# Attention scores of 64-feature heads as two 64-row matmuls into two PSUM banks, keys no longer block-diagonal

## Chip, cores and metric

One core of one Trainium2 chip runs the program. The metric is the device time of one execution in microseconds; lower is better. The time before is 1701.77 us, the median of 3 runs (1701.06 to 1705.58).

## What is computed

Two transformer blocks are applied, one after the other, to 256 tokens of 1024 features, all in float32. The first block is a hybrid mixer (a chunked state-space scan beside a "forgetting" attention of 8 heads) and a mixture of 16 experts. The second block has two layers, each with a mixer of three attentions, a cross attention and a gated feed-forward. What matters here are the four attentions with heads of 64 features; a query row of 128 tokens looks at 128 or 256 keys:

```
forgetting:  logits = einsum('bqhd,bkhd->bhqk', q, k) * 64**-0.5 + fcum[q] - fcum[k]    # block 1, 8 heads
window:      s = einsum('bqgrd,bkgd->bgrqk', qb, kb) * 64**-0.5                         # block 2, each layer:
             p = masked_probs(s, mask, sink)      # SWA, window 128, with a sink        # 8 heads, 2 key groups
             o_sel, o_win                         # NSA, selected and window, gated     # 2 x 8 heads, 2 key groups
             mla_mixer: heads of 96 features      # not touched by the layout below
             x = x + merged @ w_out ; x = x + cross_attn(...) ; x = x + ffn(...)
```

With 256 tokens each attention is plain causal attention over one or two blocks of 128 keys (SWA also masks the keys that are 128 or more behind).

## The kernel before, in words

Everything is written in straight Python on one `Build` object; a scheduler then orders the instructions of each engine. It goes by the order in which they are written and by when an operand or a buffer is free in its own model, so matmuls of a later projection are put between those of an attention. Every engine then takes its own instructions strictly in that order. SBUF work tiles are pages of 4, 2 and 1 KB per partition, taken and given back in turn (`a`, `f`; `PAGES` says how many). PSUM has 8 banks: two for projections (`lin`), two for scores (`S`), one each for transposes (`tp`) and outputs (`o`), two for the rest (`m`).

Projections (`linA`, `linB`, `mm3`, L161 to L163) split each float32 operand into a high and a low float32r part and make three matmuls of it. The attention matmuls are plain float32, and the trace shows each of them as two records on TensorE.

`attn` (L391) serves one group of four heads. It makes the scores in three fills of an `S` bank: four heads for the first 128 queries (four times 128 keys), then heads 0 and 1, then heads 2 and 3 for the second 128 queries (twice 256 keys). `qkpairs` (L422) makes the scores of two heads in one matmul of 128 contraction rows (L427): the queries of two heads lie in the two halves of the partitions, and the keys stand in a block-diagonal tile, head one's keys in rows 0 to 63 of one column block, head two's in rows 64 to 127 of the next, with zeros elsewhere. The zeros are set by GpSimd (`newdiag`, L1458 and L1459; L845 and L846 in `mixer1`) and the keys are put in by two copies of ScalarE (`kdiag`, L1452 and L1453; L852 and L853). A matmul of a bf16 identity with a mask closes each fill (L407, in SWA also L405). `smax` (L352) takes row maxima (L357), exponentials with their sums (L364), reciprocals (L371) and the scaling (L374); `ptile` transposes the probabilities (L383); the outputs are matmuls of 64 columns (L416 to L418), even heads into PSUM partitions 0 to 63, odd heads into 64 to 127.

`attn` runs 18 times: 2 calls in `mixer1` (with 8-row matmuls that add the forget sums, L867), and in each layer of `mixer2` 2 for MLA, 2 for SWA and 4 for NSA. All but the four of MLA go through `qkpairs`: 14 calls with 4 matmuls each.

Of the kernel before, what the change touches and what calls it, by code (L numbers as in the profile page):

```python
# [16 lines left out]
P = 128  # L17
# [23 lines left out]
_add("stri", (_i[:, None] < _i[None, :]))  # L41
_add("iota", np.broadcast_to(_i, (P, P)))
# [6 lines left out]
_add("gidx", np.broadcast_to(np.array([0.0, 1.0, 2.0, 3.0]), (P, 4)))  # L49
# [16 lines left out]
class Build:  # L66
    PAGES = {4: 21, 2: 7, 1: 5}
# [283 lines left out]

    def smax(self, S, nh, nk, nsink=None, gate=None):  # L352

# [6 lines left out]
        page = self.a(2, "pr")  # L360
        pr = page[:, :nh * nk].rearrange("p (a b) -> p a b", a=nh)
# [30 lines left out]
    def attn(self, qk, V, out, first=True, nsink=None, gate=None, swa=False):  # L392

        nc = self.nc
        mk = lambda m, n: m.rearrange("p (a b) -> p a b", a=4)[:, 0:n, :]
        PTs = {}
        for i, heads in ((0, (0, 1, 2, 3)), (1, (0, 1)), (1, (2, 3))):
            nk = (i + 1) * P  # L400
            nh = len(heads)
            S = self.bank("S", "S")[:, :nh * nk].rearrange("p (a b) -> p a b", a=nh)
            qk(S, heads, i, nk)
            if swa and i == 1:
                nc.tensor.matmul(S[:, :, 0:P], self.identb, self.smaskb.rearrange("p (a b) -> p a b", a=2), start=False, stop=False,  # L405
                                 skip_group_check=True)
            nc.tensor.matmul(S[:, :, i * P:nk], self.identb, mk(self.cmaskb, nh), start=False, stop=True, skip_group_check=True)  # L407
            h0 = heads[0]
            page, pr = self.smax(S, nh, nk, None if nsink is None else nsink[:, h0:h0 + nh], None if gate is None else gate(i, h0, nh))
            PTs[i, h0] = self.ptile(pr, nh, i + 1, "s" if h0 else "v")  # L410
            self.f(page)
        o = out()
        for h in range(4):
            q = o[(h % 2) * 64:(h % 2) * 64 + 64, h // 2, :]
            P0, P1 = PTs[0, 0][1], PTs[1, h // 2 * 2][1]
            nc.tensor.matmul(q[:, 0:P], V(h, 0), P0[:, h, :], start=first and h < 2, stop=True, skip_group_check=True)  # L416
            nc.tensor.matmul(q[:, P:T], V(h, 0), P1[:, h % 2, 0:P], start=False, stop=False, skip_group_check=True)
            nc.tensor.matmul(q[:, P:T], V(h, 1), P1[:, h % 2, P:T], start=False, stop=True, skip_group_check=True)  # L418
        for page, _ in PTs.values():
            self.f(page)  # L420
# [93 lines left out]
    def setup2(self):  # L514
# [6 lines left out]
        self.tri, self.stri, self.iota = self.C("tri"), self.C("stri"), self.C("iota")  # L521
# [30 lines left out]
    def setup3(self):  # L552
        nc, cp = self.nc, self.cp
        mp, rr, r1, rd, d8 = self.late
        b16 = cp.tile([P, 11 * P], BF, name="b16")
        nc.vector.tensor_copy(b16[:, 0:P], self.ident)
        self.identb = b16[:, 0:P]
        o = P
        for i, (m, n) in enumerate((("cmask", 4), ("smask", 2), ("dmask", 4))):
            v = b16[:, o:o + n * P]  # L560
            nc.vector.tensor_copy(v.rearrange("p (a b) -> p a b", a=n), bc(mp[:, i * P:(i + 1) * P], 1, n))
            setattr(self, m + "b", v)
            o += n * P
# [16 lines left out]
    def ropetables(self):  # L580
# [4 lines left out]
        ang = self.small([P, 2, 48], "ang", 1)  # L585
        for t in range(2):
            nc.vector.tensor_scalar(ang[:, t, :], C("invf"), pf[:, t:t + 1], None, op0=ALU.mult)
        k = self.small([P, 2, 48], "kk", 1)
# [11 lines left out]
        sn = self.small([P, 2, 48], "sn", 1)  # L600
# [13 lines left out]
        self.rt = rt  # L614

# [119 lines left out]
    def mixer1(self):  # L735
# [56 lines left out]
        az = self.small([P, 2, 24], "az", 1)  # L792
        nc.vector.scalar_tensor_tensor(az, z, -1.0, z, op0=ALU.mult, op1=ALU.max)
        e = self.small([P, 2, 24], "e", 1)
        nc.scalar.activation(e, az, AF.Exp, scale=-1.0)
        w = self.small([P, 2, 24], "w", 1)
# [3 lines left out]
        w2 = self.small([P, 2, 24], "w2", 1)  # L800
        nc.vector.tensor_mul(w2, w, w)
        pl = self.small([P, 2, 24], "pl", 1)
# [6 lines left out]
        nc.vector.scalar_tensor_tensor(sp, pl, 2.0, z, op0=ALU.mult, op1=ALU.add)  # L809
        nc.scalar.activation(self.Aneg, self.alog, AF.Exp)  # L810
# [31 lines left out]
        kbp = [self.a(4, f"kbd{j}") for j in range(2)]  # L842
        kbd = [k.rearrange("p (a b c) -> p a b c", a=2, b=2) for k in kbp]
        for k in kbd:
            nc.gpsimd.memset(k[0:64, :, 1, :], 0.0)  # L845
            nc.gpsimd.memset(k[64:P, :, 0, :], 0.0)  # L846
# [13 lines left out]
        for g in range(2):  # L860
            pairs = self.qkpairs(lambda p, g=g: qT[:, 2 * g + p, :], lambda p, g=g: kbd[g][:, p, :, :])

            def qkf(S, heads, i, nk, g=g):
# [1040 lines left out]
```

## Time and profile before

| | |
|---|---|
| median of the runs | 1701.77 us |
| the profiled execution | 1705.38 us |
| its span, first to last instruction | 1703.6 us |
| TensorE busy with matmuls | 1605.4 us, 94% |
| VectorE / ScalarE / GpSimd busy | 992.9 / 737.2 / 230.5 us |
| score matmuls of 64-feature heads (L427) | 112 records of 9272 |

The span is read in stages: about 0 to 105 us the start, to 430 us the rest of `mixer1` (its attention at 110 to 135), to 700 us the experts, then two layers of which the first has its attentions at about 735 to 830 us and the second at about 1245 to 1355 us. Busy times are unions of records; a matmul's record runs some 0.17 us longer than it holds the array, so the pace of TensorE is read from start to start.

### The profile page before, as it was taken

The numbers are of one execution on the slowest core, as the hardware profiler recorded it, in microseconds if no ns is written. First come the engines' busy times: TensorE is split into PE (matmuls) and PEld (weight loads), VectorE is DVE, ScalarE is ACT, GpSimd is POOL, SyncE is SP. The second block draws the span as 40 slices with busy tenths as digits, with TensorE's granted clock in tenths as the row PEclk, the third lists the DMA queues.
The fourth block names the chain that finished last, engine by engine and source line by source line (L and its number), as shares of the span: only waits on it lengthen the run. The fifth ranks groups of instructions, "written<-read, shape, count | busy, mean of one in ns | idle before, by whom it ended". The sixth has DMA issues, their size and how long they took to land. (4 is left out here: it accounts for less than half of the span.)

```text
span 1703.6 us, 23516 instructions
## 1 busy us (share of the span) xinstructions
PE 1605.4 (94%) x9272; PEld 1258.5 (74%) x9288; DVE 992.9 (58%) x1505; ACT 737.2 (43%) x1282; POOL 230.5 (14%) x258
## 2 busy tenths in 40 slices
PE   6599999988999888999999999999999999999998
PEld 5579888774433236877787789987877787789986
DVE  7866775773121128677647665545777647655544
ACT  3345754341110004565444544444565544544433
POOL 3498331420000002100000000000100000000000
PEclk9798999997999999999999999999999999999999
DMA  9867256754999997634155536554524155545550
GB/s 308 302 198 254 89 166 216 244 168 168 415 385 410 362 416 276 200 93 150 53 185 198 185 113 195 183 196 129 189 75 150 59 188 186 184 130 180 191 180 25
DMA packets 181029, 340.51 MB, mean 200 GB/s; under 512 B 20608, under 2 KB 96496, under 8 KB 173232
## 3 DMA queue, kind: packets, MB, share of 16 engines
q1 hardware_dynamic: 176784, 331.29, 55.9%
q0 software_dynamic: 1936, 6.52, 1.1%
q8 instruction: 75, 1.23, 0.3%
q10 hardware_dynamic: 2192, 1.12, 0.3%
q14 instruction: 42, 0.34, 0.1%
HBM read 337.86 MB, written 1.05 MB: 199 GB/s over the span
## 5 line engine op out<-in xcount | busy, mean ns | idle before, releaser
L226 DVE TENSOR_TENSOR wlo<-raw,whi 128x1024 fp32r<-128x1024 f32 (+3 forms) x372 | 456.4, 1238 | 316.4 <-ACT whi L226 314.5
L226 ACT CAST whi<-raw 128x1024 fp32r<-128x1024 f32 (+3 forms) x372 | 375.1, 1021 | 384.7 <-PE psA L163 152.0
L161 PE MATMUL psB<-hTh,whi 128*128 128x256 f32 x896 | 255.8, 286 | 1.3 <-ACT eA L936 0.9
L162 PE MATMUL psB<-hTl,whi 128*128 128x256 f32 x896 | 255.1, 285 | 0.0
L163 PE MATMUL psB<-hTh,wlo 128*128 128x256 f32 x896 | 254.4, 284 | 0.8 <-DVE wlo L226 0.8
L161 PE MATMUL psA<-whi,hTh 128*128 128x512 f32 (+4 forms) x496 | 188.5, 380 | 2.6 <-ACT sg L977 1.9
L163 PE MATMUL psA<-whi,hTl 128*128 128x512 f32 (+4 forms) x496 | 187.3, 378 | 0.5 <-DVE hTl L226 0.5
L162 PE MATMUL psA<-wlo,hTh 128*128 128x512 f32 (+4 forms) x496 | 186.4, 376 | 0.0
L161 PEld LDWEIGHTS psB<-hTh,whi 128*128 128x128 f32 x896 | 172.2, 192 | 3.8 <-ACT eA L936 1.3
L163 PEld LDWEIGHTS psB<-hTh,wlo 128*128 128x128 f32 x896 | 172.1, 192 | 1.7 <-DVE wlo L226 1.1
L162 PEld LDWEIGHTS psB<-hTl,whi 128*128 128x128 f32 x896 | 171.9, 192 | 2.0 <-issue 1.9
L161 PEld LDWEIGHTS psA<-whi,hTh 128*128 128x128 f32 x496 | 93.8, 189 | 20.5 <-ACT sg L977 2.3
L163 PEld LDWEIGHTS psA<-whi,hTl 128*128 128x128 f32 x496 | 93.7, 189 | 19.0 <-issue 2.4
L162 PEld LDWEIGHTS psA<-wlo,hTh 128*128 128x128 f32 x496 | 93.8, 189 | 16.0 <-issue 0.7
L364 ACT ACTIVATE pr<-S,nm 128x256 f32<-128x256 f32 (+1 forms) x160 | 66.3, 426 | 59.6 <-DVE nm L357 42.1
L639 POOL TENSOR_TENSOR macc<-macc,wmod 128x512 f32<-128x512 f32 x59 | 91.4, 1551 | 1.8
L1259 DVE TENSOR_TENSOR yf<-yg,gt 128x512 f32<-128x512 f32 x16 | 11.0, 690 | 108.8 <-PE yg L1309 93.7
L162 PE MATMUL pd<-wlo,hhl 128*128 128x512 f32 x176 | 69.8, 397 | 0.0
L163 PE MATMUL pd<-whi,hhl 128*128 128x512 f32 x176 | 69.6, 395 | 0.0
L161 PE MATMUL pd<-whi,hhl 128*128 128x512 f32 x176 | 69.3, 396 | 0.0
L272 POOL TENSOR_SCALAR sse<-ssq 128x1 f32<-128x1 f32 x16 | 4.2, 262 | 443.8 <-ACT xn L270 432.6
L638 POOL TENSOR_SCALAR wmod<-wmod,cact 128x512 f32<-128x512 f32 x59 | 60.4, 1030 | 7.6 <-DMA wmod<-in_w_mod 7.6
(583 smaller groups left out, 2987.9 us busy)
## 6 DMA issues: line engine op xcount, KB each, us to landing
raw<-in_w_in SPq DMA_DIRECT2D x62, 1024.0 KB, 5.1
raw<-in_w_down SPq DMA_DIRECT2D x44, 1024.0 KB, 7.5
raw<-in_w_gate_up SPq DMA_DIRECT2D x44, 1024.0 KB, 5.1
wmod<-in_w_mod SPq DMA_DIRECT2D x48, 512.0 KB, 5.0
raw<-in_w_gate SPq DMA_DIRECT2D x22, 1024.0 KB, 8.3
wx<-in_w_up SPq DMA_DIRECT2D x32, 512.0 KB, 10.2
raw<-in_w_up SPq DMA_DIRECT2D x16, 1024.0 KB, 9.9
wx<-in_w_gate SPq DMA_DIRECT2D x20, 512.0 KB, 9.9
```

Of the source, the lines that this page charges most:

```text
L161: m(out, l[0], r[0], start=start, stop=False)
L162: m(out, l[0], r[1], start=False, stop=False)
L163: self.lastmm = m(out, l[1], r[0], start=False, stop=stop)
L226: return self.nc.scalar.copy(hi, src), self.nc.vector.tensor_sub(lo, src, hi.bitcast(F32))
L272: self.nc.gpsimd.tensor_scalar(sq[2], sq[1][:, 0:1], 1.0 / D, RMS_EPS, op0=ALU.mult, op1=ALU.add)
L364: le = nc.scalar.activation(pr[:, h, :], S[:, h, :], AF.Exp, bias=nm[:, h:h + 1], accum_out=den[:, h:h + 1])
L638: e.tensor_scalar(w, w, c, 1.0, op0=ALU.mult, op1=ALU.mult)
L639: return e.tensor_add(acc, acc, w)
L1259: nc.vector.tensor_mul(yp, y[n], gt[:, n * 512:(n + 1) * 512])
```

## The change

The keys lie in a plain tile, as the queries do: heads with even numbers in partitions 0 to 63, heads with odd numbers in 64 to 127. `qkrows` makes one matmul of 64 contraction rows for each head, and writes even heads (b = 0) into one `S` bank and odd heads (b = 1) into the other. A call of `attn` with `rows=True` therefore takes both `S` banks for the first 128 queries and both again for the second 128; the first fill is masked and normalised in two halves, which share one page of probabilities. MLA keeps the old path. `newdiag`, `kdiag` and their memsets and second copies go; the key tiles of a layer take 2 KB pages in place of 4 KB ones, and `PAGES` has 9 of 2 KB in place of 7. Masks are kept once in bf16 and repeated by a stride of zero, some small tiles move into pages, and the strict triangle of the expert ranks is dropped (its sum now counts the token itself).

```diff
-    PAGES = {4: 21, 2: 7, 1: 5}
+    PAGES = {4: 21, 2: 9, 1: 5}
...
-        for i, heads in ((0, (0, 1, 2, 3)), (1, (0, 1)), (1, (2, 3))):
...
-            S = self.bank("S", "S")[:, :nh * nk].rearrange("p (a b) -> p a b", a=nh)
-            qk(S, heads, i, nk)
...
+        for i, sets in ((0, ((0, 2, 1, 3),)), (1, ((0, 2), (1, 3)))) if rows else ((0, ((0, 1, 2, 3),)), (1, ((0, 1), (2, 3)))):
+            nk = (i + 1) * P
+            gt = gate(i) if gate else None
+            if rows:
+                SS = [self.bank("S", "S")[:, :2 * nk].rearrange("p (a b) -> p a b", a=2) for b in range(2)]
+                qk(SS, (0, 1, 2, 3), i, nk)
+                for S in SS:
+                    close(S, i, 2)
+            for n, heads in enumerate(sets):
+                nh = len(heads)
+                if rows and i == 0:
+                    page = self.a(2, "pr")
+                    pr = page.rearrange("p (a b) -> p a b", a=4)
+                    for b in range(2):
+                        self.smax(SS[b], 2, nk, nsink[:, b:4:2] if nsink is not None else None, gt[:, b:4:2] if gate else None, pr[:, 2 * b:2 * b + 2, :])
+                elif rows:
+                    page, pr = self.smax(SS[n], 2, nk, nsink[:, n:4:2] if nsink is not None else None, gt[:, n:4:2] if gate else None)
...
-    def qkpairs(self, qT, kbd):
+    def qkrows(self, qT, kT):
 
         def qk(S, heads, i, nk):
-            for n, p in enumerate(sorted({h // 2 for h in heads})):
-                self.nc.tensor.matmul(S[:, 2 * n:2 * n + 2, :], qT(p)[:, i * P:(i + 1) * P], kbd(p)[:, :, 0:nk],
-                                      start=n == 0, stop=False, skip_group_check=True)
+            for p in range(2):
+                for b in range(2):
+                    c = slice(b * 64, b * 64 + 64)
+                    self.nc.tensor.matmul(S[b][:, p, :], qT(p)[c, i * P:(i + 1) * P], kT(p)[c, 0:nk], start=p == 0, stop=False,
+                                          skip_group_check=True)
...
-                nc.scalar.copy(kbd[b - 2][0:64, :, 0, :], ps[0:64])
-                nc.scalar.copy(kbd[b - 2][64:P, :, 1, :], ps[64:P])
+                nc.scalar.copy(kT[:, 2 * b - 4:2 * b - 2, :], ps)
...
-        self.kdiag(k, dst, t)
+        pt = self.bank("m", "tpk")[:, :T].rearrange("p (a b) -> p a b", a=2)
+        for g in range(2):
+            self.nc.tensor.transpose(pt[:, g, :], k[:, g * P:(g + 1) * P], self.ident)
+        self.nc.scalar.copy(dst.rearrange("p (a b) -> p a b", a=2)[:, :, t * P:(t + 1) * P], pt)
...
-        kaD = self.newdiag("kaD")
+        kaD = self.a(2, "kaD")
...
-        ksD, kwD = self.newdiag("ksD"), self.newdiag("kwD")
+        ksD, kwD = self.a(2, "ksD"), self.a(2, "kwD")
```

The new order of the instructions shows what the scheduler makes of it. On TensorE, in `mixer1`, the first call of `attn` stood like this before (S_915, S_941 are the first two fills of scores, kbd0 the block-diagonal keys, cfT the forget sums, b16 the identity and masks):

```order
L427 MATMUL S_915<-kbd0_602,qT_601 128x256 x2
L867 MATMUL S_915<-cfT_585,idt_70 128x128 x4
L407 LDWEIGHTS b16_542
L407 MATMUL S_915<-b16_542 128x512
L427 MATMUL S_941<-kbd0_602,qT_601 128x512
L867 MATMUL S_941<-cfT_585,idt_70 128x256 x2
```

and stands like this now (S_902 and S_903 are the two banks of the first 128 queries, S_938 and S_939 those of the second; where "..." stands, two rows like the two above it are left out, then again two, one weight load, and last 16 matmuls of the next projection):

```order
L451 MATMUL S_902<-kT_596,qT_595 128x128
L451 MATMUL S_903<-kT_596,qT_595 128x128
...
L880 MATMUL S_902<-cfT_579,idt_70 128x128
L880 MATMUL S_903<-cfT_579,idt_70 128x128
...
L406 MATMUL S_902<-b16_542 128x256
L406 LDWEIGHTS b16_542
L406 MATMUL S_903<-b16_542 128x256
...
L451 MATMUL S_938<-kT_596,qT_595 128x256 x2
L451 MATMUL S_939<-kT_596,qT_595 128x256 x2
L383 MATMUL tp_931<-idt_70,pr_914 128x128 x2
```

Here the matmuls of the two banks follow each other, without another instruction between them. On TensorE, in the NSA attention of the first layer (the window keys kwD, first 128 queries; pcmp is a small 64-row product, tp a transpose of probabilities), the order before was:

```order
L427 MATMUL S_8194<-kwD_7681,brT_7799 128x256
L1700 MATMUL pcmp_8078<-w2_8015,sv8_8076 128x64
L427 MATMUL S_8194<-kwD_7681,brT_7799 128x256
L383 MATMUL tp_8152<-idt_70,pr_8144 128x128 x4
L407 LDWEIGHTS b16_542
L407 MATMUL S_8194<-b16_542 128x512
```

and it is now, at the same fill (S_8238 and S_8239 are the two banks; psA1 is a projection):

```order
L451 MATMUL S_8238<-kwD_7718,brT_7832 128x128 x2
L406 LDWEIGHTS b16_542
L406 MATMUL S_8238<-b16_542 128x256
L159 MATMUL psA1_8512<-whi_8519,hTh0_6618 128x512
L160 MATMUL psA1_8512<-wlo_8520,hTh0_6618 128x512
L451 MATMUL S_8239<-kwD_7718,brT_7832 128x128 x2
L383 MATMUL tp_8199<-idt_70,pr_8191 128x128 x4
L406 LDWEIGHTS b16_542
L406 MATMUL S_8239<-b16_542 128x256
```

Here the two banks come apart: the even heads are done, masked and followed by a projection before the odd heads begin. Outside the attentions the order of TensorE, VectorE, ScalarE and GpSimd is that of before, but for a few weight loads in `mixer1` that change places.

## Rows read from the trace of the kernel before

**Rows 1.** The page: busy time, and the span in 40 slices.
```profile
PE 1605.4 (94%) x9272; PEld 1258.5 (74%) x9288; DVE 992.9 (58%) x1505; ACT 737.2 (43%) x1282; POOL 230.5 (14%) x258
...
PE   6599999988999888999999999999999999999998
...
PEclk9798999997999999999999999999999999999999
DMA  9867256754999997634155536554524155545550
```
**Rows 2.** Busy time by stage: window, its length, engines (records), clock, DMA share, GB/s.
```profile
105.00:165.00 60.00, 58.99 (x382) 49.35 (x382) 37.62 (x51) 30.48 (x64) 51.84 (x43) 0.94 0.62 200
...
720.00:820.00 100.00, 97.94 (x631) 75.92 (x636) 74.40 (x180) 61.02 (x176) 4.39 (x8) 1.00 0.37 119
...
1240.00:1360.00 120.00, 117.95 (x766) 88.67 (x770) 88.75 (x207) 66.11 (x197) 2.18 (x3) 1.00 0.31 98
```
**Rows 3.** One line: the score matmuls, duration ns min/median/max, forms (rows*columns).
```profile
L427 PE MATMUL S<-kaD,qaT x32: 377/486/697, 748.6 to 1269.8; 128*128 128x256 f32 x16, 128*128 128x512 f32 x16
...
L427 PE MATMUL S<-kwD,brT x32: 379/537/697, 806.5 to 1345.2; 128*128 128x256 f32 x16, 128*128 128x512 f32 x16
...
L427 PE MATMUL S<-kbd,qT x16: 378/487/592, 110.1 to 127.1; 128*128 128x256 f32 x8, 128*128 128x512 f32 x8
```
**Rows 4.** Timeline, NSA: start us, us, engine, line; a row merges its records.
```profile
796.40 1.03 PE L427 MATMUL S<-ksD,brT 128*128 128x256 f32 x4
...
797.75 1.02 PE L427 MATMUL S<-ksD,brT 128*128 128x512 f32 x2
```
**Rows 5.** One line: the 8-row matmuls of the forget sums.
```profile
L867 PE MATMUL S<-cfT,idt x32: 270/373/478, 111.1 to 128.4; 8*128 8x128 f32 x16, 8*128 8x256 f32 x16
```
**Rows 6.** Timeline of TensorE, SWA: a projection, then output matmuls of 64 columns.
```profile
757.32 0.40 PE L162 MATMUL psA<-wlo,hTh 128*128 128x512 f32 x1
757.56 0.40 PE L163 MATMUL psA<-whi,hTl 128*128 128x512 f32 x1
757.79 0.40 PE L161 MATMUL psA<-whi,hTh 128*128 128x512 f32 x1
758.12 0.32 PE L417 MATMUL oT<-PT,va 128*64 128x128 f32 x1
758.13 0.32 PE L416 MATMUL oT<-PT,va 128*64 128x128 f32 x1
758.28 0.27 PE L417 MATMUL oT<-PT,va 128*64 128x128 f32 x1
758.29 0.27 PE L416 MATMUL oT<-PT,va 128*64 128x128 f32 x1
758.39 0.27 PE L418 MATMUL oT<-PT,va 128*64 128x128 f32 x1
758.40 0.27 PE L417 MATMUL oT<-PT,va 128*64 128x128 f32 x1
```
**Rows 7.** Timeline of TensorE, NSA: 64-row matmuls (L1700) between 128-row ones.
```profile
806.06 0.49 PE L383 MATMUL tp<-idt,pr 128*128 128x128 f32 x3
...
806.50 0.60 PE L427 MATMUL S<-kwD,brT 128*128 128x256 f32 x2
807.03 0.43 PE L1700 MATMUL pcmp<-w,sv 64*128 64x64 f32 x2
807.39 0.70 PE L427 MATMUL S<-kwD,brT 128*128 128x256 f32 x2
807.92 0.27 PE L383 MATMUL tp<-idt,pr 128*128 128x128 f32 x1
```
**Rows 8.** Timeline, SWA: from a closed fill of scores to its last exponential.
```profile
750.15 0.69 DVE L357 TENSOR_REDUCE nm<-S 128x4 f32<-128x512 f32 x1 [0.42 <-PE S L427]
...
751.15 0.37 ACT L364 ACTIVATE pr<-S,nm 128x128 f32<-128x128 f32 x1 [0.91 <-DVE nm L359]
...
751.51 0.36 ACT L364 ACTIVATE pr<-S,nm 128x128 f32<-128x128 f32 x1
```
**Rows 9.** Timeline of VectorE: one operation of 512 and one of 256 columns.
```profile
789.08 0.69 DVE L1426 TENSOR_TENSOR ra<-qb,rt 128x512 f32<-128x512 f32 x1
...
790.65 0.42 DVE L1433 TENSOR_TENSOR qb<-ra,rb 128x256 f32<-128x256 f32 x1
```
**Rows 10.** By line: the reciprocals; the bf16 masks (busy us, mean ns).
```profile
L407 PE MATMUL S<-b 128*128 128x256 bf16 (+1 forms) x40 | 11.4, 286 | 0.0
...
L371 DVE RECIPROCAL rd<-den 128x2 f32<-128x2 f32 (+1 forms) x62 | 10.2, 165 | 8.3 <-ACT pr L364 7.8
```
**Rows 11.** One line each: a zeroing of a key tile, one of its two copies.
```profile
L1458 POOL MEMSET kaD<- x2: 518/518/519, 681.8 to 1187.8; 64x512 f32 x2
...
L1452 ACT COPY kaD<-tpk x4: 364/365/366, 747.3 to 1258.0; 64x256 f32<-64x256 f32 x4
```

More of the change, by code (lines that the diff above doesn't have):

```diff
@@ L349, in bcast, with smax @@
         return t
[L352 removed]
+    def smax(self, S, nh, nk, nsink=None, gate=None, pr=None):
         nc = self.nc
@@ L404, in attn @@
             if swa and i == 1:
[L405 to L409, printed above, removed]
@@ L410, in attn @@
-            PTs[i, h0] = self.ptile(pr, nh, i + 1, "s" if h0 else "v")
-            self.f(page)
+                nc.tensor.matmul(S[:, :, 0:P], self.identb, bc(self.smaskb, 1, nh), start=False, stop=False, skip_group_check=True)
+            nc.tensor.matmul(S[:, :, i * P:nk], self.identb, bc(self.cmaskb, 1, nh), start=False, stop=True, skip_group_check=True)
+        for i, sets in ((0, ((0, 2, 1, 3),)), (1, ((0, 2), (1, 3)))) if rows else ((0, ((0, 1, 2, 3),)), (1, ((0, 1), (2, 3)))):
[9 more added lines that the diff above has]
+                if rows and i == 0:
+                    page = self.a(2, "pr")
+                    pr = page.rearrange("p (a b) -> p a b", a=4)
[3 more added lines that the diff above has]
+                    page, pr = self.smax(SS[n], 2, nk, nsink[:, n:4:2] if nsink is not None else None, gt[:, n:4:2] if gate else None)
+                else:
+                    S = self.bank("S", "S")[:, :nh * nk].rearrange("p (a b) -> p a b", a=nh)
+                    qk(S, heads, i, nk)
+                    close(S, i, nh)
+                    h0 = heads[0]
+                    page, pr = self.smax(S, nh, nk, nsink[:, h0:h0 + nh] if nsink is not None else None, gt[:, h0:h0 + nh] if gate else None)
+                q, PT = self.ptile(pr, nh, i + 1, "s" if n else "v")
+                for m, h in enumerate(heads):
+                    (P1 if i else P0)[h] = PT[:, m, :]
+                pages.append(q)
+                self.f(page)
@@ L584, in ropetables @@
         nc.vector.tensor_copy(pf, self.pi)
-        ang = self.small([P, 2, 48], "ang", 1)
+        page = self.a(2, "rtmp")
+        ang, k, sn = [page[:, i * 96:(i + 1) * 96].rearrange("p (a b) -> p a b", a=2) for i in range(3)]
         for t in range(2):
             nc.vector.tensor_scalar(ang[:, t, :], C("invf"), pf[:, t:t + 1], None, op0=ALU.mult)
-        k = self.small([P, 2, 48], "kk", 1)
         MAGIC = 12582912.0
@@ L614, in ropetables @@
         self.rt = rt
+        self.f(page)
     def modps(self, j, n, acc, late=False):
@@ L790, in mixer1 @@
         nc.vector.tensor_scalar(z[:, :, 16:24], z[:, :, 16:24], -1.0, None, op0=ALU.mult)
-        az = self.small([P, 2, 24], "az", 1)
+        page = self.a(1, "spt")
+        az, e, w, w2, pl = [page[:, i * 48:(i + 1) * 48].rearrange("p (a b) -> p a b", a=2) for i in range(5)]
         nc.vector.scalar_tensor_tensor(az, z, -1.0, z, op0=ALU.mult, op1=ALU.max)
-        e = self.small([P, 2, 24], "e", 1)
         nc.scalar.activation(e, az, AF.Exp, scale=-1.0)
-        w = self.small([P, 2, 24], "w", 1)
         nc.vector.tensor_scalar(w, e, 2.0, None, op0=ALU.add)
@@ L841, in mixer1 @@
         qT = v4(qTp)
[L842 to L846, printed above, removed]
+        kTp = self.a(4, "kT")
+        kT = v4(kTp)
         for b in range(4):
```

88 lines of the change are left out of this document (31 added, 57 removed).

## The prediction, made before the run

> **What bounds the kernel now.** I read the page first. TensorE is busy 94% of the span, and every other engine 58% or less; the slices show TensorE at 8 or 9 tenths throughout [rows 1]. So a change pays or costs where it lengthens or shortens TensorE's own stream, or makes TensorE wait. Then the stages with the 14 calls that change: in the two attention stretches of the layers TensorE is busy for 97.94 of 100 us and 117.95 of 120 us at a granted clock of 1.00, VectorE for 74.40 and 88.75, ScalarE for 61.02 and 66.11; in the stretch of `mixer1` it is 49.35 of 60 at 0.94 [rows 2]. The reader is to see that TensorE is fed there: the projections that the scheduler puts between the attention's steps cover what the other engines do.
>
> A record's duration is not what it holds the array for, so I take the pace from merged rows. Four records of 256 columns last 1.03 us together [rows 4] and one alone 0.377 at least [rows 3]: (1.03 - 0.38)/3 = 0.216 us from start to start. Two of 512 columns last 1.02 [rows 4] and one alone some 0.59 (the longest of kbd) [rows 3]: 0.43. A float32 matmul is two records, so 0.43 us for 256 columns, 0.86 for 512. A call has two matmuls of 256 columns and two of 512: 2.59 us, and 14 calls 36.3 us. That is the whole of what the change can work on directly; there are no more than these 112 records [rows 3].
>
> **Part 1: the score matmuls.** Each matmul of 128 rows and 2n columns becomes two of 64 rows and n columns. A matmul with fewer rows is no shorter: those of 8 rows still last 270 to 478 ns [rows 5], where a transpose of 128 rows and as many columns lasts 0.27 us [rows 7]. So, one after the other, the halves take the same 36.3 us, and the gain is only what the two halves overlap. That two parts of the array can run side by side is shown for column halves: output matmuls of 64 columns start in pairs 0.01 us apart (758.12 and 758.13, 758.28 and 758.29) [rows 6]. For row halves no row shows it; I take it to hold where the two halves stand next to each other in the order, as those pairs do, and nothing where another matmul stands between. In the new order the 112 matmuls stand in 56 groups, because the two banks come free one after the other and the scheduler fills each as it does. The halves meet in both fills of one call in `mixer1` (0.43 + 0.86 = 1.30 us saved), and in each layer at the first fill of one SWA call (where only one of the two heads of each bank meets its partner, 0.22) and at both fills of one NSA call (0.43 + 0.86): 1.51 each. Together -1.30 - 2 x 1.51 = **-4.3 us**; bounds 0 (no overlap) and -4.3.
>
> The Trainium skill, TensorEngine Tiling (Array Packing), section Theoretical Speedup, gives up to 2x for a small dimension of 64 or less; on all 28 fills that would be half of 36.3, -18.1 us. No row here shows it for row halves; I weigh it as the first rival.
>
> **Part 2: changes of tile size.** Between equal shapes the array goes on without a gap: projections follow each other at 0.23 us (757.32, 757.56, 757.79) [rows 6], transposes at (0.49 - 0.27)/2 = 0.11 [rows 7]. A 64-row matmul between 128-row ones does not. The stretch from 806.50 to 807.92 [rows 7] holds two L427 matmuls of 256 columns (0.43 each) and one L1700 of 64 rows (two records of 0.11): 1.08 us of work in 1.42, so the visit to the other tile size costs some 0.33 us. Its parts: L427 holds the array till 806.93 and L1700 starts at 807.03, a gap of 0.10. L1700's second record starts 0.43 - 0.27 = 0.16 after its first, 0.05 later than the pace, and so ends at 807.30; the next L427 starts at 807.39, a gap of 0.09; and its second record starts 0.70 - 0.38 = 0.32 after its first, 0.10 late. Now the 56 groups are each such a visit. Counted in the two orders, tile sizes change 226 times before and 318 now, 92 more, nearly all in the layers, or 46 visits net (some groups touch another 64-row matmul, or stand where a change was already). What a visit costs lies between the two gaps alone, 0.19, and 0.39 if a late record of 0.10 comes on both sides. Most groups are followed by a bf16 mask or a projection, not by a float32 matmul that loads its weights, so I take 0.30, nearer to the visit measured than to the gaps alone: 46 x 0.30 = **+13.8 us**; bounds 8.7 and 17.9. TensorE's stream is the bound there [rows 2], so all of it is path.
>
> The Trainium skill, same page, section Key Properties, says that a change of tiling mode drains TensorE, and states no price. The trace agrees with the rule: the 0.09 and 0.10 us on either side of L1700 [rows 7] are such gaps.
>
> **Part 3: masks and their loads.** Each of the 14 calls closes four banks, not three: 14 more bf16 matmuls, the columns in all the same. The array time is unchanged; a weight load more may show by the 0.1 us of a late start: 14 x 0.035 = **+0.5 us**, bounds 0 and 1.4. The mask rows are 286 ns each at present [rows 10].
>
> **Part 4: VectorE, ScalarE, GpSimd.** The first fill's normalising is split in two: 256 columns for 0.42 against 512 for 0.69 [rows 9], 0.15 more for each, in the maxima, the scaling and some products, and one more reciprocal of 0.165 [rows 10] per call: some 0.7 us x 14 = 10 us on VectorE, 4 to 5 in each stretch of 100 to 120 us where it has 25 to 31 idle [rows 2]. Cost nothing, by that cover; without it, up to 10. The 14 dropped key copies give ScalarE 14 x 0.36 = 5 us, the 16 dropped memsets of 0.518 [rows 11] 8 us of GpSimd, busy 14% [rows 1]: nobody was held by them, so no gain.
>
> **Part 5: the banks.** A call fills two banks twice, where it filled three in turn. The second pair must wait until the exponentials of the first are done: from a row maximum that starts at 750.15 to the end of the second exponential, 751.51 + 0.36, is 1.7 us for the first two heads [rows 8]. Two heads per bank now need that long per bank, not for four. In `mixer1`'s new order 16 matmuls of a projection stand between, in SWA some 8 of 0.23, 1.9 us [rows 6], so the wait is covered: **0**; bounds 0 and 0.5 us for each of the 14 calls, 7.
>
> **Part 6: order elsewhere.** In `mixer1` some weight loads change places on SP's queue. The stretch has 62% of DMA time in use and GpSimd is done long before [rows 2], so 0.
>
> **Sum.** +13.8 - 4.3 + 0.5 = **+10.0 us** to the profiled execution of 1705.38 (span 1703.6 and 1.8 around it), which lies 3.6 above the median of the runs, 1701.77. Against that median I forecast 1701.77 + 10.0 = **1711.8 us**. About what a measurement of this kernel can tell from no change is 0.3%, 5.1 us: faster is below 1696.7, slower above 1706.9.
>
> **Rivals.** *Halves overlap everywhere (the other side).* If matmuls on different row halves run side by side even when a mask or a transpose stands between, at all 28 fills, -18.1 us comes in, and if a visit costs only the gaps, +8.7 + 0.5 remain: -8.9, 1692.9 us. It decides at L451 in the layers: it needs the odd half to start before what precedes it has ended. Against it: matmuls are taken in order, and the L1700 of another tile size starts only after its predecessor is through [rows 7]. Even with all overlap it falls to -4 at 0.30 per visit. Chance 0.07.
>
> *Cheap visits.* The gaps alone, with the adjacent overlaps: 8.7 - 4.3 + 0.5 = +4.9, 1706.7 us, no change by 0.3%. For it: groups here are longer than that one of L1700, and the late records may hide behind a bf16 mask. Chance 0.22.
>
> *The change doesn't do what it says.* Row halves never run side by side, even adjacent: 13.8 + 0.5 = +14.3, 1716.1 us. For it: no row of before shows them doing so. Chance 0.15.
>
> *Banks.* The second pair waits 0.5 us per call: +7, 1718.8 us. For it: four fills on two banks, and VectorE has 74 to 75% of the stretch filled [rows 2], so that a split chain can queue behind other work. Against it: the projections that stand there. Chance 0.12.
>
> **How the numbers follow.** The forecast's own case has the remaining 0.44. The range of 8 in 10 takes in cheap visits with their lower end and the banks' case: the low end is the cheap case, 1706.7, less some 5 us towards the first rival and for the spread of the runs (1701.06 to 1705.58), 1701; the high end is 1720, beyond which lie dear visits (17.9) with no overlap and waits together. Faster than 0.3%: the first rival, with a little for a mishap of the clock, 0.08. Within it: the cheap visits mostly, 0.22. Slower: forecast, no overlap and banks, 0.70.
>
> **What would show it.** In the profile after, L451 in `mixer1`'s first call should start in pairs some 0.01 us apart, and in the layers alone. Around each group of L451 there should be gaps of some 0.1 us on both sides, and the layers' stretches should become some 4 to 5 us longer each with TensorE as busy as before. L451 should wait for ScalarE's exponentials for less than 7 us in all. VectorE's busy time should rise by some 10 us and ScalarE's fall by some 5. I am wrong if the stretches get shorter, which would mean overlap across other work, or if L451's idle time is tens of microseconds, which would mean the banks.

## The result and the profile after

The changed kernel takes 1726.62 us (median of 4 runs, 1721.72 to 1730.7), the kernel before 1702.31 (4 runs, 1701.06 to 1705.58): ratio 1.0139, 95% interval 1.0107 to 1.0171. The forecast, 1711.8 us, had the sign and 40% of the loss; the time lies above its range (1701 to 1720).

The profiled execution of the changed kernel is the quickest of its four, 1721.72 us with a span of 1719.7, and that of before, 1705.38, was near the slowest of its own, so the two traces differ by 16.1 us where the medians differ by 24.3. The page, as in [rows 1], reads:

```profile
PE 1631.2 (95%) x9414; PEld 1284.3 (75%) x9414; DVE 987.1 (57%) x1565; ACT 732.2 (43%) x1272; POOL 222.0 (13%) x242
...
PE   5899999979999888999999999999999999999998
...
PEclk9798999999999999999999999999999999999999
```

TensorE's matmuls and weight loads are busy 26 us longer each; no other engine is. The windows of [rows 2] (columns as there):

```profile
105.00:165.00 60.00, 56.37 (x352) 48.89 (x351) 36.86 (x53) 25.93 (x59) 54.79 (x48) 0.86 0.55 179
720.00:820.00 100.00, 98.54 (x659) 76.76 (x658) 72.44 (x191) 56.48 (x164) 2.31 (x4) 1.00 0.35 108
1240.00:1360.00 120.00, 118.54 (x799) 90.37 (x796) 85.51 (x225) 65.97 (x200) 2.17 (x3) 1.00 0.31 94
```

Fixed windows hold other work now, so a layer is better measured between two places of the program: its first MLA score matmul (not touched by the change) and the first matmul of its output projection. The first starts of both, by line, before and after:

```profile
L1546 PE MATMUL S<-kmT,qmT x64: 273/326/382, 727.2 to 1248.0; 96*128 96x128 f32 x32, 96*128 96x256 f32 x32
...
L161 PE MATMUL psA<-whi,oaTh x32: 395/396/396, 910.6 to 1429.7; 128*128 128x512 f32 x32
```

```profile
L1544 PE MATMUL S<-kmT,qmT x64: 273/326/382, 724.2 to 1254.8; 96*128 96x128 f32 x32, 96*128 96x256 f32 x32
...
L159 PE MATMUL psA<-whi,oaTh x32: 392/396/400, 914.0 to 1443.0; 128*128 128x512 f32 x32
```

910.6 - 727.2 = 183.4 us before, 914.0 - 724.2 = 189.8 after; with starts to two places it is 183.38 and 189.87, 6.5 us more in each layer, 13.0 in both. In these two kernels this **stretch** is the same in the second layer to 0.1 us, and it serves as the yardstick below; its windows, before and then after:

```profile
727.20:910.60 183.40, 181.31 (x1050) 140.32 (x1055) 117.66 (x234) 97.91 (x238) 4.18 (x8) 1.00 0.38 124
```

```profile
724.20:914.00 189.80, 188.37 (x1110) 145.91 (x1109) 119.45 (x262) 96.26 (x234) 2.88 (x5) 1.00 0.38 120
```

TensorE's busy time grows by 7.1 us, more than the stretch: its idle time shrinks from 2.1 to 1.4. So this is more work on TensorE, not waiting. VectorE grows by 1.8 only. What the score matmuls do shows in the timeline of TensorE, first in `mixer1`, where the halves stand together:

```profile
101.57 0.39 PE L161 MATMUL psA<-whi,hTl 128*128 128x512 f32 x1
101.89 0.71 PE L451 MATMUL S<-kT,qT 64*128 64x128 f32 x8
102.54 1.15 PE L880 MATMUL S<-cfT,idt 8*128 8x128 f32 x8
```

and in the NSA attention, at the fill of the order above where they stand apart:

```profile
809.37 0.39 PE L161 MATMUL psA<-whi,hTl 128*128 128x512 f32 x1
809.69 0.71 PE L451 MATMUL S<-kwD,brT 64*128 64x128 f32 x4
810.33 0.28 PE L406 MATMUL S<-b 128*128 128x256 bf16 x1
810.37 0.48 PE L159 MATMUL psA<-whi,hTh 128*128 128x512 f32 x1
810.69 0.40 PE L160 MATMUL psA<-wlo,hTh 128*128 128x512 f32 x1
811.01 0.71 PE L451 MATMUL S<-kwD,brT 64*128 64x128 f32 x4
811.65 0.66 PE L383 MATMUL tp<-idt,pr 128*128 128x128 f32 x4
```

Eight records side by side last 0.71 us, and so do four alone: adjacent row halves do run together, for half the time. The Trainium skill (TensorEngine Tiling (Array Packing), Theoretical Speedup) has this factor of two; the rows agree, for halves that stand together. Apart, they pay the visit: a projection that starts at 809.37 and holds the array for 0.23 is done at 809.60, the scores start at 809.69, a gap of 0.09. Four records hold the array for 0.43, to 810.12, but the mask starts at 810.33, 0.21 later: together 0.30 us, as much as Part 2 of the prediction takes for a visit. The Trainium skill, same page, section Key Properties, says that a change of tiling mode drains TensorE; the gap of 0.09 us agrees with it, as in [rows 7].

There is a second loss, where nothing was changed. In the feed-forward the psB projections follow each other without a gap, so a window of one length counts them; the view is windows of psB alone, 1030 to 1120 us, before and after:

```profile
1030.00:1120.00 90.00, 90.00 (x774) 90.00 (x773) 5.43 (x8) 4.70 (x8) 1.00 0.58 191
```

```profile
1030.00:1120.00 90.00, 90.00 (x752) 90.00 (x751) 4.76 (x7) 4.74 (x8) 1.00 0.57 184
```

774 matmuls in 90 us before, 752 after, at the same granted clock of 1.00: 0.1163 and 0.1197 us each, 2.9% more for the same instruction. With 3 x 896 of them in the kernel that is, by estimate, some 9 us.

### The profile page after: what moved, and what is told of

The parts are those of the page before. It is cut to its first block, busy times and chain, and to the rows that moved or that the text cites. A ratio compares the mean times of both kernels' runs of the same rounds, so it can differ in the third digit from the quotient of the medians.

```text
span 1719.7 us, 23811 instructions
## 1 busy us (share of the span) xinstructions
PE 1631.2 (95%) x9414; PEld 1284.3 (75%) x9414; DVE 987.1 (57%) x1565; ACT 732.2 (43%) x1272; POOL 222.0 (13%) x242
## 5 line engine op out<-in xcount | busy, mean ns | idle before, releaser
L159 PE MATMUL psB<-hTh,whi 128*128 128x256 f32 x896 | 260.6, 291 | 0.3 <-DVE xbc L899 0.3
L160 PE MATMUL psB<-hTl,whi 128*128 128x256 f32 x896 | 259.4, 290 | 0.0
L161 PE MATMUL psB<-hTh,wlo 128*128 128x256 f32 x896 | 258.0, 288 | 0.8 <-DVE wlo L224 0.8
L161 PEld LDWEIGHTS psB<-hTh,wlo 128*128 128x128 f32 x896 | 175.8, 196 | 1.8 <-DVE wlo L224 1.1
L658 POOL TENSOR_TENSOR macc<-macc,wmod 128x512 f32<-128x512 f32 x59 | 87.7, 1490 | 1.7
L355 DVE TENSOR_REDUCE nm<-S 128x2 f32<-128x512 f32 (+2 forms) x76 | 43.6, 587 | 30.2 <-PE S L406 23.9
```

The costliest lines, as they stand in the source:

```text
L159: m(out, l[0], r[0], start=start, stop=False)
L160: m(out, l[0], r[1], start=False, stop=False)
L161: self.lastmm = m(out, l[1], r[0], start=False, stop=stop)
L355: nc.vector.tensor_reduce(nm, S, axis=AX.X, op=ALU.max, negate=True)
L658: return e.tensor_add(acc, acc, w)
```

## Experiments

Each ratio is to the kernel before on the same chip; the runs come from several chips, so ratios are compared rather than medians. "Stretch" and "clock" are the length and the mean granted clock of TensorE in the first layer's stretch of the profiled run, psB the count in the 90 us where it was read.

| run | median us | ratio to before (95%) | stretch us | clock | psB |
|---|---|---|---|---|---|
| the change | 1726.6 | 1.0139 (1.0107 to 1.0171) | 189.9 | 1.00 | 752 |
| e1_pages256 | 1716.1 | 1.0084 (1.0057 to 1.0111) | 189.5 | 1.00 | 774 |
| e2_before64 | 1712.0 | 1.0058 (1.0036 to 1.0081) | 183.8 | 1.00 | 752 |
| e3_fullrows | 1712.4 | 1.0064 (1.0041 to 1.0087) | 185.8 | 1.00 | |
| e4_together | 1720.6 | 1.0106 (1.0083 to 1.0129) | 190.9 | 0.98 | |
| e5_bypair | 1710.1 | 1.0057 (1.0035 to 1.0079) | 183.6 | 1.00 | |
| e6_outpairs | 1731.5 | 1.0170 (1.0146 to 1.0193) | 193.2 | 0.98 | |
| e7_scan | 1720.2 (one run) | | 191.2 | 0.99 | 763 |
| e8_half | 1716.6 | 1.0091 (1.0066 to 1.0117) | 188.6 | 1.00 | |
| e9_halftog | 1707.7 | 1.0039 (1.0022 to 1.0056) | 188.7 | 0.98 | |
| e10_three | 1728.7 | 1.0154 (1.0127 to 1.0181) | 185.7 | 1.00 | |
| e11_distance | 1720.8 | 1.0126 (1.0104 to 1.0149) | 189.5 | 1.00 | 774 |
| e12_rest | 1702.1 | 1.0013 (1.0002 to 1.0025) | 183.1 | 1.00 | |
| e13_mixrows | 1704.1 | 1.0016 (1.0006 to 1.0027) | 183.1 | 1.00 | |
| e14_mixjoin | 1700.4 | 0.9988 (0.9976 to 1.0001) | 183.1 | 1.00 | |
| e15_fulljoin | 1707.0 | 1.0028 (1.0013 to 1.0044) | 183.2 | 1.00 | |

**Where the pages lie: e1_pages256, e2_before64, e7_scan, e11_distance.** The smaller constants and tables of the change shift every work page from 256 to 64 modulo 512 bytes of a partition. One unused tile moves them back, in the pool that lies just ahead of the pages:

```diff
+            self.sm.tile([P, 48], F32, tag="pad", bufs=1, name="pad")
             self.setup()
```

> The changed kernel with 192 bytes of padding in front of the work pages, so that each page starts at 256 modulo 512 bytes of a partition, as before the change, and not at 64; nothing else moves. In the trace of the change each matmul of the psB projections takes 0.120 us from start to start, before it 0.117, in every stage. Theory A (the pages' place sets that pace): the pace returns to 0.117 us, and with 2688 such matmuls times 3.3 ns the time falls by 6 to 9 us from the change's 1726.6, to about 1719. Theory B (the pace comes from the new order or from the code, not from the place): pace 0.120 and the time as with the change, 1722 to 1731.

The reverse in the kernel before: the same tile, and the table `sn` taken out of that pool into a page.

> The kernel before, with one small table in a page in place of a tile of its own and padding, so that pages start at 64 modulo 512 bytes, as in the changed kernel. Theory A: psB matmuls go from 0.117 to 0.120 us, and the time rises by 6 to 9 us over the kernel before, to about 1709 to 1711. Theory B: pace 0.117 and the time that of before, 1702.

psB's windows of e1_pages256 and of e2_before64:

```profile
1030.00:1120.00 90.00, 90.00 (x774) 90.00 (x773) 5.43 (x8) 4.74 (x8) 1.00 0.58 191
```

```profile
1030.00:1120.00 90.00, 90.00 (x752) 90.00 (x751) 5.45 (x8) 4.73 (x8) 1.00 0.55 183
```

The count goes back to 774 in the one and falls to 752 in the other, and the time goes with it: -10.5 us between the medians (-0.55% by the ratios) and +9.3 us (+0.58%). Theory A holds both ways: the place costs 9 to 10 us. To see which operand's place it is, the eight buffers of split weights were spread 64 bytes apart (`[P, 1040]` in place of `[P, 1024]` for `hi`, `lo` and `wx`), the pages left at 256:

> The changed kernel with pages at 256 modulo 512 bytes (as e1_pages256) and the eight buffers of split weights placed 64 bytes apart modulo 512 (32 to 480), so that one run shows the pace of projections whose moving operand is the split weights (512 columns, 0.2333 us so far, all at 224) by its place, and that of psB, whose stationary operand they are. If the place of the moving operand sets the pace: psA matmuls differ between buffers by some 3%, 0.233 to 0.240 us, and psB stay at 0.1167. If it is the place of both or of the stationary one: psB differ by buffer. If only the distance between pages and the rest matters: no difference by buffer.

```profile
1030.00:1120.00 90.00, 90.00 (x763) 90.00 (x762) 5.45 (x8) 4.72 (x8) 1.00 0.57 187
```

763 in the window, between the two. The pages, psB's moving operand, had not moved, so the stationary operand's place counts too, and it counts buffer by buffer. Set beside the addresses of the built kernel, two neighbouring psB matmuls start 0.117 us apart where the weights of both lie at 224 (32 bytes under the pages, as before the change) and 0.120 where they lie at 416 (160 above them, as in the change). The one run's time is not used. The last run of this group moves both operands by the same amount, against the kernel before:

```diff
+            self.cp.tile([P, 80], F32, name="padc")
+            self.sm.tile([P, 48], F32, tag="pad", bufs=1, name="pad")
```

> The changed kernel with its pages where the change puts them, at 64 modulo 512 bytes, but with the buffers of the raw and split weights moved from 224 to 32, so that the weights start 32 bytes below a page again, as before the change (224 and 256), and not 160 above. Theory D (the distance of the two operands of a matmul sets the pace of psB): pace 0.1167 us, the whole 10 us below the change's 1726.6, about 1716, as e1_pages256. Theory M (the place of the moving operand by itself, at 64): pace 0.120 us, the whole as the change's, 1726.

```profile
1030.00:1120.00 90.00, 90.00 (x774) 90.00 (x773) 5.44 (x8) 4.72 (x8) 1.00 0.58 190
```

774 with pages at 64: Theory D for the pace. The time did not follow as forecast: 5.8 us between the medians, but only 0.13% by the ratios (2 us), with an interval that overlaps those of both e1_pages256 and the change. From the first MLA score to the end its profile takes 987.6 us, as that of e1_pages256 (987.4) and 8 less than that of the change (995.5). What is missing lies ahead of the layers: its first MLA score starts at 729.8 us, that of the change at 724.2; why is open. By what rule the distance sets the pace (-32 bytes is quick, +160 is slow) is left open too.

**Row tiles, and heads by parity: e3_fullrows, e5_bypair, e12_rest.** Block-diagonal keys, with their memsets and second copies, come back; the two banks and all else stay as in the change:

```diff
-                    c = slice(b * 64, b * 64 + 64)
-                    self.nc.tensor.matmul(S[b][:, p, :], qT(p)[c, i * P:(i + 1) * P], kT(p)[c, 0:nk], start=p == 0, stop=False,
+                    self.nc.tensor.matmul(S[b][:, p, :], qT(p)[:, i * P:(i + 1) * P], kT(p)[:, b, 0:nk], start=p == 0, stop=False,
```

> The changed kernel with its two banks and four closings per call, but with block-diagonal keys again: each of the 112 score matmuls has 128 rows of which 64 are zeros (memsets and second copies are back), so there are no changes of tile size for the scores and no overlap of row halves. Pages lie as in the change. Theory 1 (the attentions' loss is 46 visits to another tile size, less the overlap): the two attention stretches lose some 10 of the 12.7 us that they gained, the whole is 1726.6 - 10 = about 1717. Theory 2 (the loss is the banks' rotation, the split maxima and the extra masks): the stretches stay as with the change, the whole about 1726.

The stretch falls by 4.1 us to 185.8, 8.2 in two layers: that is what row tiles cost net. But 2.0 us over e2_before64 stay (183.8, pages at the same place). The outputs looked different. With full rows any two heads can share a bank (the order of heads in `attn` goes with it):

```diff
-                    self.nc.tensor.matmul(S[b][:, p, :], qT(p)[:, i * P:(i + 1) * P], kT(p)[:, b, 0:nk], start=p == 0, stop=False,
+                    self.nc.tensor.matmul(S[p][:, b, :], qT(p)[:, i * P:(i + 1) * P], kT(p)[:, b, 0:nk], start=b == 0, stop=False,
```

> The run with block-diagonal keys and full rows (e3_fullrows) again, but with heads 0 and 1 in one bank and heads 2 and 3 in the other, as the fills of the kernel before had them; four fills per call as in the change. In e3_fullrows a layer's stretch from its first MLA score to its output projection still takes 185.78 us, against 183.80 with before's fills on pages at the same place, and the output matmuls take 18.64 against 17.20 us of it, with 61 pairs of column halves side by side in place of 71. Theory P (heads grouped by parity make the even heads' probabilities ready before the odd ones', so output matmuls of 64 columns lose their partners): 71 pairs and 17.2 us again, the stretch about 184.4, the whole 2 to 3 us below e3_fullrows' 1712.4. Theory Q (the second fill per bank or the split maxima cost it): stretch stays at 185.8, the whole 1712.

The stretch is 183.6 us: 2.2 per layer come from heads by parity and the order that goes with it. The timeline of TensorE at the outputs of the first SWA call, e3_fullrows:

```profile
757.07 0.38 PE L441 MATMUL oT<-PT,va 128*64 128x128 f32 x2
757.38 0.70 PE L450 MATMUL S<-kaD,qaT 128*128 128x256 f32 x2
758.01 0.32 PE L440 MATMUL oT<-PT,va 128*64 128x128 f32 x1
758.02 0.32 PE L439 MATMUL oT<-PT,va 128*64 128x128 f32 x1
...
758.72 0.38 PE L440 MATMUL oT<-PT,va 128*64 128x128 f32 x2
758.93 0.38 PE L441 MATMUL oT<-PT,va 128*64 128x128 f32 x2
```

and of e5_bypair:

```profile
757.95 0.27 PE L441 MATMUL oT<-PT,va 128*64 128x128 f32 x1
757.97 0.27 PE L440 MATMUL oT<-PT,va 128*64 128x128 f32 x1
...
758.82 0.27 PE L440 MATMUL oT<-PT,va 128*64 128x128 f32 x1
758.93 0.38 PE L441 MATMUL oT<-PT,va 128*64 128x128 f32 x2
```

A merged row "x2" is two records of one column half, one after the other: three such rows in the one, one in the other, and in e3_fullrows the call's outputs are cut in two by a fill of scores. Counted over the trace of a stretch (starts less than 0.04 us apart), the 192 output records make 61 pairs in e3_fullrows, as in the change, and 71 in e5_bypair, as before. What the outputs take of the stretch (windows of the tile PT on TensorE, e3_fullrows and e5_bypair):

```profile
722.60:908.30 185.70, 18.12 (x192) 1.00 0.38 123
723.40:907.00 183.60, 16.89 (x192) 1.00 0.40 124
```

The pairs thus account for 1.2 of the 2.2 us; where the rest goes is not shown. The whole runs put e5_bypair 0.07% under e3_fullrows, within the spread; the split between row tiles and parity rests on the stretches.

With the pages at 256 again, only the rest of the change is left:

> e5_bypair (block-diagonal keys and full rows, heads 0 and 1 in one bank and 2 and 3 in the other, all else as in the change) with the pages back at 256 modulo 512 bytes: what is left of the change are the two banks filled twice, the fourth closing of each call, the split maxima, the masks repeated by a stride of zero, the tables in pages and the changed order of weight loads. If visits to other tile sizes, heads grouped by parity and the place of the pages are the whole loss: the time of before, 1700 to 1703, and a layer's stretch of 183.4 us. Each us above is what the remaining edits cost.

1702.1 us, 0.13% above before, and a stretch of 183.1: the second filling of two banks, the fourth mask, the split maxima, the strided masks and the changed order of loads cost 0 to 4 us together. Of the 1.39%, 0.55 are the place (the change less e1_pages256) and 0.71 row tiles and parity (e1_pages256 less e12_rest). Such differences along a chain of runs add up by themselves; what closes the account is that only 0.13 is left at its end. The profiles say the same where they repeat best, from the first MLA score to the end: 995.5 us in the change, 987.3 without row tiles (e3_fullrows), 982.9 without parity too (e5_bypair), 974.9 with the pages back (e12_rest), 976.4 before. That is 8.2, 4.4 and 8.0 us, and -1.5 for the rest; 19.1 in all. The other 5 of the 24.3 us between the medians lie ahead of the layers, and no kept profile shows them: the change's is its quickest run, and reaches its first MLA score 3.0 us earlier than that of before.

**Trying to mend it: e6_outpairs, e8_half, e4_together, e9_halftog, e10_three.** e6_outpairs issues the second block's outputs of odd heads first and the even ones after (`for h in (1, 0, 3, 2)`, behind the first odd one).

> The changed kernel, whose output matmuls of the second 128 queries are issued for an odd head first and only then for the even ones, so that neighbours in column halves are ready together. Theory P: output matmuls go from 18.6 to some 17.2 us per layer's stretch, which goes from 189.86 to about 188.4, less what the later start of the even heads costs; the whole 2 to 3 us under the change's 1726.6. If they are no cause, 189.9 and 1726.

A miss: 3.4 us more per stretch, and only 56 pairs. Yet the outputs take 16.3 us of it, not 18.1, as Theory P asks. What grew is TensorE's idle time, from 1.4 to 3.6 us, and its granted clock is 0.98, not 1.00; below, such a clock is worth some 3 us. So the run doesn't refute that the outputs were a cause. e8_half keeps row tiles but writes the rotated queries in another order, so that bank 0 holds heads 0 and 1:

> The changed kernel with pages at 256 modulo 512 bytes, and with the queries of the window attentions written in another order, so that heads 0 and 1 of a group lie in partitions 0 to 63 and heads 2 and 3 in 64 to 127: the two banks then hold heads 0 and 1, and 2 and 3, as the fills of the kernel before did, while row tiles stay. Four small vector operations a layer and token block more. Theory P (grouping heads by parity costs 2.2 us per layer, shown between e3_fullrows and e5_bypair): stretch of a layer 189.48 - 2.2 = 187.3 us, the whole 1716.1 (e1_pages256) - 4.4 = about 1712. If with row tiles that is no cost: 189.5 and 1716.

71 pairs again, but 0.9 us gained, not 2.2, at a median like e1_pages256's. TensorE's busy time fell by 1.6 us (187.96 in e1_pages256, 186.40 here), its idle time rose from 1.4 to 2.2; 0.8 of it is one projection's wait for a copy of ScalarE (`vs`). Whether the added vector operations cause that wasn't tried. In e4_together (on the change) and e9_halftog (on e8_half) the first matmul of a fill waits for both banks:

```diff
+            first = one(S, i, nk, 0, 0)
+            for e in self.lastexps:
+                self.tc.add_manual_dep(first.ins, e.ins.name, mybir.DependencyInfo(mybir.DependencyClass.Sync, mybir.DependencyReason.DATA), reason="pair")
```

> The changed kernel with one wait more for each fill: its first matmul waits for the last exponentials of both banks, so that even and odd heads stand next to each other in the order (some 23 of 28 pairs of 256 columns and 20 of 28 of 128 columns are adjacent, against 8 and 12 half-way so far; 309 changes of tile size against 318). Theory 1 (adjacent halves overlap, visits cost 0.3 us): overlap of 13 to 14 us in place of 4.3 and 4 visits fewer, 10 to 11 us off the change's time, about 1716, less what the added waits cost. Theory 3 (row halves gain nothing because the waits or the weight loads stand in the way): as with the change, 1726, or slower.

> e8_half with the wait of e4_together (the first score matmul of a fill waits for the last exponentials of both banks), so that halves stand next to each other; 293 changes of tile size against 318. In e4_together the scores themselves fell from 19.34 to 14.03 us a layer, but the stretch rose from 189.9 to 190.9, as transposes, outputs and idle time rose by 7. Theory W (those waits are the banks': two banks can't be filled before both are read): the stretch is about 1 us above e8_half's again, 188 to 189, the whole 1713 to 1716. Theory P alone (the loss came mostly from outputs that wait for the odd heads): stretch 184 to 185, the whole 1706 to 1708.

The first layer's stretches stay, 190.9 against 189.9 and 188.7 against 188.6. TensorE's busy time in e4_together's is shorter, but it waits:

```profile
719.20:910.10 190.90, 186.41 (x1110) 144.87 (x1109) 121.25 (x262) 95.66 (x234) 2.89 (x5) 0.98 0.37 119
```

4.5 us idle (190.90 - 186.41) against 1.4 in the change, and a clock of 0.98 where it was 1.00. So the overlap comes, and two things take it back, waits and the clock. What the clock takes can be read in e9_halftog, whose two layers differ in it:

```profile
722.85:911.59 188.74, 184.20 (x1111) 143.63 (x1109) 121.38 (x266) 95.60 (x234) 2.88 (x5) 0.98 0.38 121
1236.44:1423.63 187.19, 182.66 (x1110) 142.32 (x1109) 121.33 (x266) 95.61 (x234) 2.73 (x4) 0.99 0.39 124
```

The first has two spells at the lower of the clock's two levels (1.2 GHz, not 2.4), from 770.6 and from 808.1 us, the second has one. TensorE is idle for 4.5 us in both, so the 1.55 us between them are the price of a spell; e7_scan, with one spell in its first layer and none in its second, gives 1.56. Ahead of the first spell TensorE had just waited 1.66 and 0.97 us; ahead of the other two it had been busy. By this estimate both layers of e9_halftog would take 185.6 us at the full clock, 3 less than e8_half's, which has no such spell. A third bank for scores, in place of one of the two for other transposes, asks whether the waits are for score banks:

> e9_halftog with three banks for scores and one in place of two for the rest, so that the first half of the next fill finds a free bank; 289 changes of tile size. Theory W: waits fall by half, the stretch of a layer some 2 to 3 us under e9_halftog's, if the single bank for transposes does not take it back; the whole near 1708. If it is not the score banks that are waited for: as e9_halftog or above.

```profile
749.40:935.10 185.70, 181.88 (x1118) 142.11 (x1117) 120.98 (x266) 96.91 (x237) 2.89 (x5) 1.00 0.39 124
```

The stretch falls to 185.7, but that doesn't show that they are. Of the 3.0 us, 2.3 are busy time, at a clock of 1.00 again, and the length is what the estimate gives e9_halftog without its spells. Idle time falls from 4.5 to 3.8 only, and the two longest waits of TensorE read the same in both profiles:

```profile
PE tp L385 <- DVE den L370: 1.7, 1, 1.7
PE tp L385 <- ACT kcd L1588: 1.0, 1, 1.0
```

These are transposes that wait for VectorE and ScalarE, not scores that wait for a bank. Theory W holds in that waits and what follows them take the overlap back; that they are waits for the score banks is not shown, nor why the clock stays up with the third bank. The kernel ahead of the layers, with one bank fewer for the rest, loses more than 20 us (first MLA score at 749.4 us, 722.8 in e9_halftog). No arrangement with row tiles in the layers came under the 183.4 of before.

**`mixer1`: e13_mixrows, e14_mixjoin, e15_fulljoin.** e9_halftog is 8.9 us under e8_half, and its layers show 1.3 of it (188.7 and 187.2 against 188.6 twice). Three versions of e12_rest change `mixer1` alone: row tiles, row tiles with the wait, the wait without row tiles.

> e12_rest (1702.1 us; block-diagonal keys and full rows, pages at 256) with the change's row tiles, parity banks and plain keys in the two calls of mixer1 alone. Theory H (mixer1's attention is hidden by the weights that it waits for, so that row tiles there cost and gain nothing): 1702, within 3 us. Theory X (the part of the loss that the layers' stretches don't show lies in mixer1): 4 to 6 us above, 1706 to 1708.

> e13_mixrows with the wait of e9_halftog in mixer1 alone: the first score matmul of a fill waits for the last exponentials of both banks. e9_halftog was 8.9 us below e8_half, but the two layers' stretches account for 1.3 of it. Theory J (the wait changes the order in mixer1, where the rest was gained): 6 to 8 us below e13_mixrows, 1694 to 1697 if Theory H holds, under the kernel before. Theory N (the 7 us were the spread of runs): as e13_mixrows, within 3 us.

> e12_rest with the same wait in mixer1, but full rows and block-diagonal keys there too. If the gain in mixer1 is the order (projections ahead of the attention), it is here too: 1694 to 1697. If it needs the row halves' overlap (1.3 us by the count, so not likely): 1702, as e12_rest.

Row tiles in `mixer1` cost and gain nothing (1.0016 against 1.0013). With the wait it is 0.28% less by the ratios, 3.7 us between the medians; without row tiles the wait gains nothing (1.0028). So by the medians the wait helps there together with row tiles only, and why is open: the scheduler orders the projections around each of the three in another way, and what lies ahead of the layers varies from profile to profile by several us (their first MLA score at 719 to 730 us, e10_three aside). The traces can't tell: e15_fulljoin's times spread from 1698.0 to 1711.2 us, and its profile, of a run of 1700.9, has the span of e14_mixjoin's (1699.1 and 1699.0). e14_mixjoin is the lowest of all, 0.12% under the kernel before, with an interval that just takes in no change.

## Why the prediction was wrong

**Part 1 held.** Halves that meet run side by side, eight records in the time of four; those that are apart don't. Not all that were counted meet in full: in the layers' NSA call the second fill (at 803.60 us) has two pairs of records that start together, not four, so some 1.1 of the 1.51 us come.

**Part 2 held.** The trace has 42 more changes of tile size in a layer's stretch, 21 visits; at 0.30 and less 1.51 of overlap that is 4.8 us, and undoing row tiles gave 4.1 (e3_fullrows). In `mixer1`, where 4 visits and 1.30 of overlap leave a gain of 0.1, it is nothing (e13_mixrows).

**Parts 3 and 5 held.** Idle time in the stretch fell from 2.1 to 1.4 us, and the wait of the scores (L451) for ScalarE is small:

```profile
its engine sat idle before it (us, times) until:
  issue: 10.9, 48
  ACT whi L224: 0.7, 2
  ACT es L368: 0.7, 2
  ACT pr L364: 0.3, 2
```

The 10.9 us of "issue" are pauses of the weight loads, which waited for nothing that the profile shows.

**Part 4 failed in what it left out.** VectorE's 10 us were priced too high (1.8 per stretch) and rightly hidden (e12_rest). But the part asked only how long the split operations last, not for whom: banks by parity make even heads ready before odd ones, and the outputs of [rows 6] need one of each to run in pairs. Not in the sum: +2.2 us per layer, 4.4 in all (e3_fullrows less e5_bypair). That parity costs it is shown; that the lost pairs do is shown for 1.2 of the 2.2. The rows and the new order were both there to be read for it.

**Part 6 failed.** It counted DMAs for the changes "elsewhere" and gave the smaller tables and other `PAGES` no term, as if an edit that moves no instruction could not move the time. They move addresses, and 2688 unchanged matmuls became 2.9% slower: +9 to 10 us (e1_pages256, e2_before64), the largest single term. No row of before could have priced it, for only one placing was seen; but a bound for it was owed, and a range without one was too narrow.

So the sum was +8.2 (forecast 10.0, with `mixer1`) for what it looked at, +4.4 and +9 to 10 for what it did not; together some 22 of 24.3 us, the rest within the spread of the runs. Of the rivals none was right: halves that never run side by side and halves that overlap across other work are refuted by the timeline, the cheap visits by the 0.30 us of a visit there and by e3_fullrows, the banks by e12_rest. Of the signs named in advance, pairs in `mixer1`, gaps of 0.1 us, less than 7 us of waiting and ScalarE's -5 us came; the stretches grew by 6.5 us, not 4 to 5, and VectorE's total fell by 5.8.

## What to carry to other kernels

Splitting an array into row tiles pays only where the halves meet in the order: count, in the built order, the visits to another tile size and the pairs that stand together, and price a visit (0.3 us here) against half the matmul. When heads are regrouped, look at the next consumer that relies on pairs. And where a diff changes the size of anything that lies ahead of the work buffers, pad it back before judging the change, since placement alone was worth 0.6% here. Compare the granted clock of a stretch before calling a difference in its length a wait.

## What the runs showed of the hardware

- The pace of a matmul of 256 columns, both operands in SBUF, depends on where they start relative to each other: 774 in 90 us where the weights start 32 bytes under a 512-byte step from the pages, 752 where they start 160 above; the same place of both shifted together (e11_distance) keeps 774, and in e7_scan the two distances give 0.117 and 0.120 us side by side in one trace.
- Row halves into two banks run together at full pace, eight records of 128 columns in 0.71 us; four alone take 0.71 too. Apart from its partner, a visit of such a half to the other tile size cost 0.30 us.
- Making both halves stand together brought the overlap and lost it again: TensorE's idle time in the stretch rose from 1.4 to 4.5 us, and spells at 1.2 GHz came, each worth 1.55 us there (e9_halftog's two layers, two spells and one).
